# Hybrid decoder block on one core: down-weight sums moved to the up phase, seven down entries taken early, first norm's gains spread by TensorE

## The chip, the core and the metric

The kernel runs on one core of a Trainium2 chip. The metric is the device time of one execution in microseconds. Three runs of the kernel before gave 1432.56, 1430.29 and 1428.49 us; the median is 1430.29 us.

## What is computed

One decoder layer on 1024 tokens of width 1024, with 16 meta tokens put in front (L = 1040). All of it is float32. Cut to what matters here:

```
h  = concat(meta, x)
xn = rmsnorm(h) * g_attn                       # first norm
proj = xn @ w_in                               # q, k, v of 4 differential and 8 stick-breaking heads
h  = h + heads(proj) @ w_out                   # attention, per-head norms, output projection
u  = rmsnorm(h) * g_ffn @ w_up                 # 2 x 2816 columns: gate and up
c  = conv_b + causal depthwise conv3(u)
h  = h + (silu(c_gate) * c_up) @ w_down        # 2816 -> 1024
out = (rmsnorm(h) * g_final)[16:]
```

## The kernel before

Each float32 factor is split into a high part (rounded for the fast matmul) and a low part (the rest); a product is three matmuls, high x high, high x low and low x high. ScalarE makes the high part by a copy, GpSimd or VectorE the low part by a subtraction. All transfers are issued on SyncE's queue. The order of instructions on each engine is fixed when the kernel is built: a list scheduler takes, in a simulation, the instruction traced first among those that are ready, and `tc.issue_after(x)` keeps an instruction behind x on its engine.

**First norm and first projections** (`first_unit`, `first_norm`, L220 to L231). Nine row tiles (a meta tile of 16 rows, eight of 128) are loaded; SyncE loads g_attn broadcast to 128 partitions (512 KB, L372) between them. Each tile gets its square sum (ScalarE, L224), `rstd` (L151 to L156), a multiply by rstd and g_attn, and a transposition with a split into xT_hi and xT_lo (L180, L183, L184). Six tiles are multiplied by one VectorE instruction (L230); tiles 3, 5 and 7 (`POOL_X`) by GpSimd with g_attn (L227) and by VectorE with rstd (L228). The projections of unit 0 (L297) run after tiles 0 to 2, 3 to 5 and 6 to 8. Values are transposed through the two banks of tag "tr".

**Attention phase.** Projection of the next unit and attention of the current one are interleaved by a written planner. `load_w` (L251) loads an input weight into one of two raw buffers and splits it. With the fourth to twelfth weight it also calls `sum_down` (L267), once for each of the nine pairs of down-weight tiles: two loads of 512 KB into the same two raw buffers, four GpSimd subtractions of 512 columns (L274 to L277), two stores of 512 KB into down_sums. These are the sums of weight blocks that a seven-product scheme for a 2 x 2 block product needs.

**Up phase** (loop over ff from 3 to 21, 19 steps). A step computes gate and up columns of one 128-wide tile with the same seven-product scheme: products `a11, a12, s2, s3, s1, a22, s4` (L1063), each 4 x 3 x 2 matmuls of 258 columns. Four weight entries a step are split by `prepare`: `load_up` loads two raw tiles (512 KB each) and forms sums ta and tb on GpSimd (L1041 to L1044); `split_w` makes high (ScalarE, L907) and low part (GpSimd, L908) in three buffers dh, dl. Convolution taps run on ScalarE and VectorE (L915, L917). Gated tiles, and sums of them (`gated_sums`, L1093 to L1099), are stored as blocks (L1087).

**Down phase.** After the last step's gates (`rest`, `gated_sums`) the pools are closed, the bank pool psd and the pool ph opened, and twelve entries taken. `take(k)` loads 256 KB of blocks and 256 KB of weight (from w_down or down_sums, L1181, L1182) into one of eight raw buffers, copies the high part (L1189), and subtracts the low part, half on GpSimd, half on VectorE (L1191). Entries 0 to 2 of each twelve use dh and dl, the others eh and el in ph. Three pairs form a group; a chain of 36 matmuls of 512 columns (L1221) uses three entries, the group's first chain entry by entry, and after each chain three more are taken. Four plain rows and the last norm follow (L1239, L1243).

Of the kernel before, what the change touches and what calls it, by code (L numbers as in the profile page):

```python
# [44 lines left out]
SUMS_FROM = 4  # L45
# [7 lines left out]
POOL_X = (3, 5, 7)  # L53
# [16 lines left out]
def f(ap):  # L70
    return ap.bitcast(F32)
# [25 lines left out]
def hybrid_block(ctx: ExitStack, tc: tile.TileContext, x, meta, g_attn, w_in, lq1, lk1, lq2, lk2,  # L97
# [8 lines left out]
    def bank(tag):  # L106
        return psum.tile([P, 512], F32, tag=tag, name=f"ps_{tag}", bufs=2)
# [89 lines left out]
    down_sums = dram.tile([N_PAIRS, 2, P, D], F32, name="down_sums")  # L197
# [12 lines left out]
    gb = pr.tile([P, D], F32, tag="aT", name="g_attn_b", bufs=3)  # L210
    rows = {}

# [6 lines left out]
    def first_norm(t):  # L219
        t0, n = tok_span(t)  # L220
        xt = rows[t]
        ss = pr.tile([P, 1], F32, tag="ss", name="ss", bufs=4)
        junk = pn.tile([P, D], BF16, tag="yb", name="junk")
        nc.scalar.activation(junk[:n], xt[:n], AF.Square, accum_out=ss[:n])  # L224
        r = rstd(pr, ss[:n], n, "rs")
        if t in POOL_X:
            nc.gpsimd.tensor_tensor(xt[:n], xt[:n], gb[:n], op=ALU.mult)  # L227
            nc.vector.tensor_scalar(xt[:n], xt[:n], r, None, op0=ALU.mult)  # L228
        else:
            nc.vector.scalar_tensor_tensor(xt[:n], xt[:n], r, gb[:n], op0=ALU.mult, op1=ALU.mult)  # L230
        transpose_split(xt, n, [(xT_hi, xT_lo, t0, 0)], ("s", "av"))  # L231
# [19 lines left out]
    def load_w(src):  # L251
        raw = pw.tile([P, D], F32, tag="raw", name="raw", bufs=2)
        nc.sync.dma_start(raw, src)
        if len(w_taken) == 2:
            both = pk_odd.tile([P, 2, D], F32R, tag="k", name="w_v0")
            hi, lo = both[:, 0], both[:, 1]
        else:
            hi = pw.tile([P, D], F32R, tag="wh", name="wh", bufs=2)
            lo = pw.tile([P, D], F32R, tag="wl", name="wl", bufs=2)
        w_taken.append(1)  # L260
        nc.scalar.copy(hi, raw)
        nc.gpsimd.tensor_tensor(lo, raw, f(hi), op=ALU.subtract)
        if 0 <= len(w_taken) - SUMS_FROM < N_PAIRS:
            sum_down(len(w_taken) - SUMS_FROM)
        return hi, lo

    def sum_down(p):  # L267

        ff = N_ROWS + 2 * p
        r0, r1 = (pw.tile([P, D], F32, tag="raw", name="raw", bufs=2) for _ in range(2))  # L270
        for i, r in enumerate((r0, r1)):
            nc.sync.dma_start(r, w_down[P * (ff + i) : P * (ff + i + 1), :])
        b11, b12, b21, b22 = (r[:, 512 * h : 512 * h + 512] for r in (r0, r1) for h in range(2))
        nc.gpsimd.tensor_tensor(b11, b12, b11, op=ALU.subtract)  # L274
        nc.gpsimd.tensor_tensor(b12, b22, b12, op=ALU.subtract)
        nc.gpsimd.tensor_tensor(b22, b22, b11, op=ALU.subtract)
        nc.gpsimd.tensor_tensor(b21, b21, b22, op=ALU.subtract)  # L277
        for i, r in enumerate((r0, r1)):
            nc.sync.dma_start(down_sums[p, i], r)
# [86 lines left out]
    def first_unit():  # L366
# [5 lines left out]
        nc.sync.dma_start(gb, g_attn.broadcast_to([P, D]))  # L372
# [529 lines left out]

    def split_w(pool, tags, src, bufs):
        hi = pool.tile([P, D], F32R, tag=tags[0], name=tags[0], bufs=bufs)
        lo = pool.tile([P, D], F32R, tag=tags[1], name=tags[1], bufs=bufs)
        w = src.shape[-1]
        nc.scalar.copy(hi[:, :w], src)  # L907
        nc.gpsimd.tensor_tensor(lo[:, :w], src, f(hi)[:, :w], op=ALU.subtract)  # L908
        return hi, lo
# [191 lines left out]

    prepare(0)
    prepare(1)
    rest = sums_of = before = None
    for ff in range(PLAIN, NF):
# [4 lines left out]
        prepare(k + 2)  # L1110
        w = ready.pop(k)
# [17 lines left out]
        prepare(k + 4)  # L1129
        w = ready.pop(k + 2)  # L1130
# [7 lines left out]
        if sums_of:  # L1138
            gated_sums(*sums_of)
            sums_of = None  # L1140
        prepare(k + 5)
# [13 lines left out]
    silus = rest()  # L1155
    gated_sums(*sums_of)
    banks.close()
    left_s.close()
# [3 lines left out]
    psd = banks.enter_context(tc.tile_pool(name="psd", bufs=1, space=PSUM, reuse_waits="tile"))  # L1162
# [6 lines left out]
    taken = {}  # L1169

    def take(k):
# [5 lines left out]
        if q < N_PAIRS:  # L1177
            ff = N_ROWS + 2 * q
            b11, b12, b21, b22 = (w_down[P * r : P * (r + 1), cs] for r in (ff, ff + 1) for cs in (lower, upper))
            t1, t3, t4, t2 = (down_sums[q, r, :, cs] for r in range(2) for cs in (lower, upper))  # L1180
            nc.sync.dma_start(raw[:, lower], blocks[q, i])  # L1181
            nc.sync.dma_start(raw[:, upper], (b11, b21, t2, t3, t1, t4, b22)[i])  # L1182
        else:
            ff = q - N_PAIRS
            nc.sync.dma_start(raw, w_down[P * ff : P * (ff + 1), :] if i else gated[ff])
        pool, tags, bufs = (pd, ("dh", "dl"), 3) if k % ENTRIES < 3 else (ph, ("eh", "el"), ENTRIES - 3)
# [18 lines left out]
    for k in range(ENTRIES):  # L1205
        take(k)
    with tc.issue_after(silus[0].ins), tc.issue_after(silus[1].ins):
        nc.scalar.preload_act_table_set("natural_log_exp_and_others")
# [80 lines left out]
```

## Time and profile before

| | |
|---|---|
| median of three runs | 1430.29 us (1428.49 to 1432.56) |
| the profiled execution's own time | 1427.61 us |
| its span | 1425.9 us |
| mean granted TensorE clock | 0.985 |
| TensorE matmul busy | 1347.5 us (95%) |
| VectorE busy | 967.8 us (68%) |
| ScalarE busy | 714.9 us (50%) |
| GpSimd busy | 749.2 us (53%) |
| share of the chain that ended last | TensorE 66%, VectorE 9% |

The span runs from the first to the last instruction; the 1.7 us between it and the execution's own time lie around it. Busy times are sums over each engine's instructions. In the rows, PE is TensorE's matmul, PEld its weight load, DVE VectorE, ACT ScalarE, POOL GpSimd, SP SyncE (SPq its queue of transfers). L numbers are lines of the kernel. A granted clock of 1.00 is 2.4 GHz, 0.50 is 1.2 GHz.

### The profile page before, as it was taken

Reading aid. Unit: us, or ns where it says so; the run is one execution under the profiler, and the core shown is the slowest. Engines: PE = TensorE matmul, PEld = TensorE weight load, DVE = VectorE, ACT = ScalarE, POOL = GpSimd, SP = SyncE. Lnnn points to the kernel's source line nnn. Section 1 sums busy time; section 2 is a strip of 40 time slices with the busy share of each in tenths; the row PEclk is TensorE's granted clock in tenths of the full one; section 3 lists DMA queues with packets and bytes.
Section 4 is the critical chain, followed back from the end, with each engine's and each line's share of the span. In section 5 each row is a group of like instructions: output and inputs, shape, how many; then the busy total and the mean of one; then the engine's idle time right before and its main releaser. Section 6 shows DMA issues by size and latency. Waiting matters only on the chain.

```text
span 1425.9 us, 24695 instructions
## 1 busy us (share of the span) xinstructions
PE 1347.5 (95%) x9000; PEld 1251.1 (88%) x9000; DVE 967.8 (68%) x1816; ACT 714.9 (50%) x1406; POOL 749.2 (53%) x769
## 2 busy tenths in 40 slices
PE   5999989999998998899999899999999996999997
PEld 5989989998987887678899899999999995888886
DVE  7377867778676787875877546555555565977755
ACT  6355655666575666542444344444454444534322
POOL 5145444235666676852103367766776573966620
PEclk9999999999999999999999999999999998999999
DMA  5154454221211127335633222323223325966502
GB/s 215 52 184 153 151 162 144 60 68 38 60 43 40 46 59 224 84 73 140 169 122 129 78 82 92 110 97 104 77 94 97 111 91 202 325 203 191 177 15 104
DMA packets 93569, 166.35 MB, mean 117 GB/s; under 512 B 11628, under 2 KB 46060, under 8 KB 93448
## 3 DMA queue, kind: packets, MB, share of 16 engines
q1 hardware_dynamic: 93448, 164.78, 37.0%
q8 instruction: 71, 1.16, 0.4%
q14 instruction: 50, 0.41, 0.1%
HBM read 111.49 MB, written 44.85 MB: 110 GB/s over the span
## 4 chain that ended last, share of the span: by engine, by line
PE 66%; DVE 9%; issue 4%; ACT 3%; POOL 2%; DMA 1%; SPq 0%; DVEq 0%; POOLq 0%; ACTq 0%
PE x L1063 27%; PE ps_x L1221 7%; PE ps_mm L297 7%; PE ps_y L1221 5%; PE ps_mm L745 5%; DVE s L501 3%; PE ps_av L588 2%; PE ps_tr L559 2%; PE ps_s L927 2%; PE ps_av L927 2%; PE ps_x L1239 2%; PE ps_y L1239 2%; PE ps_s L444 1%; PE ps_s L445 1%; PE ps_tr L180 1%
## 5 line engine op out<-in xcount | busy, mean ns | idle before, releaser
L297 PE MATMUL ps_mm<-xT_hi,wh 128*128 128x342 f32 (+7 forms) x552 | 182.6, 331 | 4.7 <-DVE qz L307 3.2
L297 PE MATMUL ps_mm<-xT_lo,wh 128*128 128x342 f32 (+7 forms) x552 | 180.1, 327 | 0.2 <-DVE xT_lo L184 0.2
L297 PE MATMUL ps_mm<-xT_hi,wl 128*128 128x342 f32 (+7 forms) x552 | 179.2, 326 | 0.0
L588 PE MATMUL ps_av<-aT,v 128*128 128x256 f32 (+3 forms) x608 | 130.8, 306 | 4.7 <-POOL aT L566 4.1
L908 POOL TENSOR_TENSOR dl<-raw,dh 128x1024 fp32r<-128x1024 f32 (+1 forms) x43 | 82.8, 1926 | 95.3 <-ACT dh L907 95.3
L1063 PE MATMUL x<-yh,dl 128*128 128x258 f32 x608 | 124.2, 286 | 0.0
L1063 PE MATMUL x<-yh,dh 128*128 128x258 f32 x608 | 123.7, 285 | 0.0
L1063 PE MATMUL x<-yl,dh 128*128 128x258 f32 x608 | 123.6, 285 | 0.0
L501 DVE TENSOR_TENSOR_SCAN s<-s 128x912 f32<-128x912 f32 (+6 forms) x72 | 100.3, 1396 | 21.8 <-POOL s L497 19.8
L1069 ACT COPY kept<-x 128x516 f32<-128x516 f32 x76 | 44.8, 590 | 135.2 <-PE x L1063 135.2
L297 PEld LDWEIGHTS ps_mm<-xT_hi,wh 128*128 128x128 f32 x552 | 105.5, 191 | 7.9 <-issue 2.4
L559 PE MATMUL ps_tr<-ident,a 128*128 128x128 f32 (+1 forms) x540 | 92.9, 277 | 18.8 <-DVE o L671 6.1
L1191 POOL TENSOR_TENSOR el<-down_raw,eh 128x512 fp32r<-128x512 f32 x53 | 91.3, 1753 | 35.9 <-ACT eh L1189 35.9
L588 PEld LDWEIGHTS ps_av<-aT,v 128*128 128x128 f32 (+2 forms) x608 | 95.2, 190 | 14.4 <-POOL aT L566 4.5
L297 PEld LDWEIGHTS ps_mm<-xT_lo,wh 128*128 128x128 f32 x552 | 105.6, 191 | 1.0 <-DVE xT_lo L184 0.5
L297 PEld LDWEIGHTS ps_mm<-xT_hi,wl 128*128 128x128 f32 x552 | 105.4, 191 | 0.3
L502 POOL TENSOR_TENSOR a<-a,s 128x912 f32<-128x912 f32 (+3 forms) x64 | 83.6, 1308 | 41.0 <-DVE s L501 33.6
L571 DVE TENSOR_TENSOR aT<-ps_tr,aT 128x512 fp32r<-128x512 f32 (+3 forms) x132 | 76.4, 585 | 34.2 <-ACT aT L570 33.4
L1063 PEld LDWEIGHTS x<-yh,dh 128*128 128x128 f32 x608 | 95.3, 191 | 0.0
L1063 PEld LDWEIGHTS x<-yl,dh 128*128 128x128 f32 x608 | 95.0, 191 | 0.0
L1063 PEld LDWEIGHTS x<-yh,dl 128*128 128x128 f32 x608 | 95.0, 191 | 0.0
L570 ACT CAST aT<-ps_tr 128x512 fp32r<-128x512 f32 (+3 forms) x132 | 66.6, 510 | 50.5 <-PE ps_tr L559 47.8
(306 smaller groups left out, 4057.5 us busy)
## 6 DMA issues: line engine op xcount, KB each, us to landing
raw<-in_w_up SPq DMA_DIRECT2D x44, 512.0 KB, 3.6
down_raw<-blocks SPq DMA_DIRECT2D x63, 256.0 KB, 3.8
raw<-in_w_in SPq DMA_DIRECT2D x24, 512.0 KB, 3.7
blocks<-cg SPq DMA_DIRECT2D x45, 256.0 KB, 3.5
raw<-in_w_down SPq DMA_DIRECT2D x18, 512.0 KB, 3.8
down_sums<-raw SPq DMA_DIRECT2D x18, 512.0 KB, 2.9
down_raw<-down_sums SPq DMA_DIRECT2D x36, 256.0 KB, 4.3
down_raw<-in_w_down SPq DMA_DIRECT2D x27, 256.0 KB, 4.1
```

What stands on the lines that cost most here:

```text
L297: nc.tensor.matmul(ps[:, :w], a[:, kt * P : (kt + 1) * P], b[:, kt, c0 : c0 + w], start=(kt == 0 and i == 0), stop=(kt == KT - 1 and i == 2))
L501: nc.vector.tensor_tensor_scan(s[:n, rev], s[:n, rev], s[:n, rev], 1.0, op0=ALU.mult, op1=ALU.bypass)
L502: (nc.gpsimd if t else nc.vector).tensor_tensor(b[:n, :keys], b[:n, :keys], s[:n, 1 : keys + 1], op=ALU.mult)
L559: pe_last[0] = nc.tensor.transpose(ps[:kn, at : at + qn], a[:qn, kk0 : kk0 + kn], ident[:qn, :qn])
L570: nc.scalar.copy(aT[:kn, 0, f0:end], ps[:kn, f0:end])
L571: nc.vector.tensor_tensor(aT[:kn, 1, f0:end], ps[:kn, f0:end], f(aT)[:kn, 0, f0:end], op=ALU.subtract)
L588: pe_last[0] = nc.tensor.matmul(av[:, :w], v[:kn, kt, vi, :], aT[:kn, ai, j * w : (j + 1) * w], start=job["count"] == 0, stop=job["count"] ...
L745: nc.tensor.matmul(ps[:n], a, b[:, hs], start=(j == 0 and i == 0), stop=(j == len(wo) - 1 and i == 2))
L908: nc.gpsimd.tensor_tensor(lo[:, :w], src, f(hi)[:, :w], op=ALU.subtract)
L1063: nc.tensor.matmul(x[:, s], w[a][:, ks], y[b][:, kt, SUB * s : SUB * s + SUB + 2], start=start and kt == 0 and i == 0, stop=kt == KT // 2 ...
L1191: engine.tensor_tensor(lo[:, cs], raw[:, cs], f(hi)[:, cs], op=ALU.subtract)
L1221: nc.tensor.matmul(ps, a[:, P * t : P * (t + 1)], b[:, upper], start=begin and j == 0 and i == 0, stop=j == n - 1 and i == 2, skip_group_c ...
```

## The change

- `sum_down` and its call go. A class `DownSums` makes the same sums in the up phase, one half of a pair (256 of 512 columns) to a step, for the 18 steps ff = 3 to 20: it loads four blocks of 128 x 256 (128 KB each) at the step's start, subtracts on GpSimd behind the split of entry k + 4, and stores four blocks before `prepare(k + 5)`. Its four buffers are those of tag "o" in pn. down_sums becomes [pair, 4, 128, 512].
- The down entries 0 to 6 (`EARLY = 7`) are taken before the last `rest` and `gated_sums`. Only right_f (the y tiles) is closed ahead of them, so ph, with the eight raw buffers and four eh and el, lies where the y tiles lay. The other five buffers (ih, il) go to a pool pi, opened on the left where the up phase's sums lay, after the last gates. The bank pool psd is opened behind all twelve.
- g_attn is loaded as one row; two float32 matmuls with a row of ones spread it into the two "tr" banks, where it stays until tile 8 is normed. All nine tiles are multiplied on VectorE, in two halves of 512 columns, each transposed behind its half.

```diff
+    def spread_gains():
+        row = pr.tile([1, D], F32, tag="aT", name="g_attn_row", bufs=3)
+        nc.sync.dma_start(row, g_attn)
+        one = pr.tile([1, P], F32, tag="vT", name="one_row", bufs=2)
+        nc.vector.memset(one, 1.0)
+        for h in range(2):
+            ps = bank("tr")
+            nc.tensor.matmul(ps, one, row[:, 512 * h : 512 * h + 512], start=True, stop=True)
+            gains.append(ps)
...
-        if t in POOL_X:
-            nc.gpsimd.tensor_tensor(xt[:n], xt[:n], gb[:n], op=ALU.mult)
-            nc.vector.tensor_scalar(xt[:n], xt[:n], r, None, op0=ALU.mult)
-        else:
-            nc.vector.scalar_tensor_tensor(xt[:n], xt[:n], r, gb[:n], op0=ALU.mult, op1=ALU.mult)
-        transpose_split(xt, n, [(xT_hi, xT_lo, t0, 0)], ("s", "av"))
+        for h, tag in enumerate(("s", "av")):
+            hs, ks = slice(512 * h, 512 * h + 512), slice(4 * h, 4 * h + 4)
+            nc.vector.scalar_tensor_tensor(xt[:n, hs], xt[:n, hs], r, gains[h][:n], op0=ALU.mult, op1=ALU.mult)
+            transpose_half(xt[:, hs], n, [(xT_hi[:, ks], xT_lo[:, ks], t0, 0)], tag)
...
-        if 0 <= len(w_taken) - SUMS_FROM < N_PAIRS:
-            sum_down(len(w_taken) - SUMS_FROM)
...
-        nc.sync.dma_start(gb, g_attn.broadcast_to([P, D]))
+        spread_gains()
...
+    class DownSums:
+        def __init__(self, step):
+            p, h = divmod(step, 2)
+            self.cols = slice(SUB * h, SUB * h + SUB)
+            self.out = down_sums[p]
+            self.b = [pn.tile([P, 342], F32, tag="o", name="b", bufs=4)[:, :SUB] for _ in range(4)]
+            for i, b in enumerate(self.b):
+                r, c = divmod(i, 2)
+                at = HD * c + SUB * h
+                nc.sync.dma_start(b, w_down[P * (N_ROWS + 2 * p + r) : P * (N_ROWS + 2 * p + r + 1), at : at + SUB])
+        def add(self):
+            b11, b12, b21, b22 = self.b
+            nc.gpsimd.tensor_tensor(b11, b12, b11, op=ALU.subtract)
+            nc.gpsimd.tensor_tensor(b12, b22, b12, op=ALU.subtract)
+            nc.gpsimd.tensor_tensor(b22, b22, b11, op=ALU.subtract)
+            nc.gpsimd.tensor_tensor(b21, b21, b22, op=ALU.subtract)
+        def store(self):
+            for i, b in enumerate(self.b):
+                nc.sync.dma_start(self.out[i, :, self.cols], b)
...
         prepare(k + 2)
+        down = DownSums(ff - PLAIN) if ff - PLAIN < 2 * N_PAIRS else None
...
         prepare(k + 4)
+        if down:
+            with tc.issue_after(split_last[0].ins):
+                down.add()
...
+        if down:
+            down.store()
         prepare(k + 5)
...
-    silus = rest()
-    gated_sums(*sums_of)
-    banks.close()
-    left_s.close()
     right_f.close()
...
-        pool, tags, bufs = (pd, ("dh", "dl"), 3) if k % ENTRIES < 3 else (ph, ("eh", "el"), ENTRIES - 3)
+        at = k % ENTRIES
+        pool, tags, bufs = (pd, ("dh", "dl"), 3) if at < 3 else (ph, ("eh", "el"), EARLY - 3) if at < EARLY else (pi[0], ("ih", "il"), ENTRIES - EARLY)
...
-    for k in range(ENTRIES):
+    for k in range(EARLY):
         take(k)
+    silus = rest()
+    gated_sums(*sums_of)
+    banks.close()
+    left_s.close()
+    pi.append(ctx.enter_context(tc.tile_pool(name="pi", bufs=1, side="left", reuse_waits="tile")))
+    for k in range(EARLY, ENTRIES):
+        take(k)
+    psd = banks.enter_context(tc.tile_pool(name="psd", bufs=1, space=PSUM, reuse_waits="tile"))
```

## Rows read from the trace of the kernel before

**Rows 1.** TensorE's waits over the span: who for whom, us total, times, longest.

```profile
PE ps_x L1221 <- ACT dh L1189: 13.0, 1, 13.0
...
PE ps_av L588 <- POOL aT L566: 4.1, 2, 2.8
...
PE ps_tr L559 <- DVE a L479: 2.5, 1, 2.5
```

**Rows 2.** Windows: stretch and length, busy us per engine (instructions), clock, DMA, GB/s.

```profile
8.00:37.00 29.00, 20.75 (x131) 19.61 (x132) 27.69 (x61) 20.77 (x51) 18.84 (x9) 1.00 0.53 198
...
60.00:240.00 180.00, 171.16 (x1147) 165.51 (x1146) 131.82 (x379) 98.49 (x224) 86.94 (x87) 0.99 0.51 161
...
850.00:1187.00 337.00, 337.00 (x2784) 337.00 (x2783) 189.22 (x263) 162.93 (x231) 220.46 (x128) 1.00 0.29 95
1187.40:1200.50 13.10, 0.09 (x1) 0.00 (x0) 6.66 (x12) 3.62 (x4) 0.00 (x0) 0.68 0.57 203
1200.50:1211.00 10.50, 10.48 (x36) 8.48 (x37) 7.25 (x7) 7.03 (x7) 9.69 (x6) 0.76 1.03 375
1211.00:1374.00 163.00, 163.00 (x721) 134.97 (x720) 128.05 (x148) 63.15 (x64) 112.27 (x66) 1.00 0.62 199
```

**Rows 3.** Chain that ended last, first down chains: start, us, what.

```profile
1200.52 10.83 PE ps_x L1221 x36
1211.35 8.16 PE ps_y L1221 x36
```

**Rows 4.** Timeline at the seam of up and down phase: start, us, engine, instruction.

```profile
1195.59 0.38 SPq L1181 DMA_DIRECT2D down_raw<-blocks  x1
...
1199.42 1.04 ACT L1189 CAST dh<-down_raw 128x1024 fp32r<-128x1024 f32 x1 [8.56 <-DMA down_raw<-in_w_down]
```

**Rows 5.** Timeline of the first norm and first projections.

```profile
7.06 1.27 DVE L230 SCALAR_TENSOR_TENSOR xt<-xt,rs,g_attn_b 16x1024 f32<-16x1024 f32 x1 [0.71 <-DMA g_attn_b<-in_g_attn]
...
10.33 1.12 PE L180 MATMUL ps_s<-ident,xt 128*128 128x128 f32 x4 [0.85 <-DVE rs L153]
...
11.75 2.64 DVE L230 SCALAR_TENSOR_TENSOR xt<-xt,rs,g_attn_b 128x1024 f32<-128x1024 f32 x1
...
16.64 2.82 DVE L228 TENSOR_SCALAR xt<-xt,rs 128x1024 f32<-128x1024 f32 x1 [0.32 <-POOL xt L227]
...
21.20 0.58 PE L297 MATMUL ps_mm<-xT_lo,wh 128*128 128x272 f32 x1
...
46.20 0.26 ACT L329 CAST v<-ps_tr 16x128 fp32r<-16x128 f32 x1
46.21 1.12 DVE L307 SCALAR_TENSOR_TENSOR qz<-ps_mm,qz 64x384 fp32r<-64x384 f32 x2 [3.10 <-ACT qz L305]
```

**Rows 6.** Transfers by issue: count, KB each, median us to landing.

```profile
gated<-c SPq DMA_DIRECT2D x12, 128.0 KB, 1.8
```

**Rows 7.** Timeline of GpSimd in the attention phase, near 205 us.

```profile
204.67 1.26 POOL L277 TENSOR_TENSOR raw<-raw 128x512 f32<-128x512 f32 x1
206.00 0.73 POOL L566 CAST aT<-aT 16x256 fp32r<-16x256 f32 x2
```

**Rows 8.** Timeline of one up step: GpSimd, SyncE's queue and TensorE.

```profile
1019.89 2.42 POOL L908 TENSOR_TENSOR dl<-raw,dh 128x1024 fp32r<-128x1024 f32 x1
1023.71 2.42 POOL L908 TENSOR_TENSOR dl<-tb,dh 128x1024 fp32r<-128x1024 f32 x1
...
1024.99 0.41 PE L1063 MATMUL x<-yh,dl 128*128 128x258 f32 x2
...
1031.02 1.29 POOL L908 TENSOR_TENSOR dl<-raw,dh 128x512 fp32r<-128x512 f32 x1 [2.55 <-ACT dh L907]
...
1031.05 0.41 PE L1063 MATMUL x<-s2h,dl 128*128 128x258 f32 x2
...
1032.34 0.33 SPq L685 DMA_DIRECT2D raw<-in_w_up  x1
...
1036.69 1.33 POOL L1041 TENSOR_TENSOR ta<-raw 128x512 f32<-128x512 f32 x1 [4.38 <-issue]
```

More of the change, by code (lines that the diff above doesn't have):

```diff
@@ L44 @@
 STAGED = 8
-SUMS_FROM = 4
+EARLY = 7
 B_EARLY = 0
@@ L52 @@
 OUT_A, OUT_B, OUT_C = range(0, 3), range(3, 6), range(6, 8)
-POOL_X = (3, 5, 7)
 COL = 0.4219
@@ L196, in hybrid_block @@
     blocks = dram.tile([N_PAIRS, 7, P, HALF], F32, name="blocks")
-    down_sums = dram.tile([N_PAIRS, 2, P, D], F32, name="down_sums")
+    down_sums = dram.tile([N_PAIRS, 4, P, HALF], F32, name="down_sums")
     left, left_out, right, right_a, right_b = (ExitStack() for _ in range(5))
@@ L209, in hybrid_block @@
     xT_lo = pl.tile([P, KT, L], F32R, name="xT_lo")
-    gb = pr.tile([P, D], F32, tag="aT", name="g_attn_b", bufs=3)
+    gains = []
     rows = {}
+    def spread_gains():
[7 more added lines that the diff above has]
+            gains.append(ps)
     def load_rows(ts_):
@@ L262, in load_w @@
         nc.gpsimd.tensor_tensor(lo, raw, f(hi), op=ALU.subtract)
-        if 0 <= len(w_taken) - SUMS_FROM < N_PAIRS:
-            sum_down(len(w_taken) - SUMS_FROM)
         return hi, lo
[L267 to L279, printed above, removed]
     w_src, w_ready, w_taken = w_in_tiles(), [], []
@@ L900, in second_norm @@
             transpose_split(yn, m, places, ("tr", "tr"))
+    split_last = [None]
     def split_w(pool, tags, src, bufs):
@@ L907, in split_w @@
         nc.scalar.copy(hi[:, :w], src)
-        nc.gpsimd.tensor_tensor(lo[:, :w], src, f(hi)[:, :w], op=ALU.subtract)
+        split_last[0] = nc.gpsimd.tensor_tensor(lo[:, :w], src, f(hi)[:, :w], op=ALU.subtract)
         return hi, lo
@@ L1154, in hybrid_block @@
         before = cg
-    silus = rest()
-    gated_sums(*sums_of)
-    banks.close()
-    left_s.close()
     right_f.close()
-    psd = banks.enter_context(tc.tile_pool(name="psd", bufs=1, space=PSUM, reuse_waits="tile"))
     ph = ctx.enter_context(tc.tile_pool(name="ph", bufs=1, side="right", reuse_waits="tile"))
@@ L1168, in hybrid_block @@
     steps += [(i, N_PAIRS + r) for r in range(N_ROWS) for i in range(2)]
-    taken = {}
+    taken, pi = {}, []
     def take(k):
@@ L1179, in take @@
             b11, b12, b21, b22 = (w_down[P * r : P * (r + 1), cs] for r in (ff, ff + 1) for cs in (lower, upper))
-            t1, t3, t4, t2 = (down_sums[q, r, :, cs] for r in range(2) for cs in (lower, upper))
+            t1, t3, t4, t2 = (down_sums[q, r] for r in range(4))
             nc.sync.dma_start(raw[:, lower], blocks[q, i])
```

## The prediction

> **What bounds the kernel now.** Three views were read. The list of TensorE's waits [rows 1] names one long wait, 13.0 us, before the first matmul of the down projection; everything else is a few microseconds. The windows [rows 2] give each stage its limit. From 8 to 37 us VectorE is busy 27.69 of 29.00 us: the first norm hangs on it. From 60 to 240 us TensorE works 171.16 of 180.00 us, so 8.8 us are lost. In the up phase TensorE is busy 337.00 of 337.00 us at clock 1.00, and GpSimd only 220.46. Between 1187.4 and 1200.5 it does nothing, its clock falls (0.68, then 0.76), and from 1211 it is full again. The chain [rows 3] prices the fall: the first 36 down matmuls take 10.83 us, the next 36 take 8.16, so 2.7 us. The timeline of the seam [rows 4] says why: the first down loads are issued at 1195.59, behind the last blocks on SyncE's queue, and the first split starts at 1199.42.
>
> **Part 1, down entries loaded early.** Seven of the twelve entries are traced ahead of the last gates. Their staging and most of their buffers lie where the four y tiles lay. A step is 168 matmuls, 20.3 us by [rows 2] (337.00 / 2784 x 168), in seven products of 2.9 us. The first y half is last read by product 2, so raw loads can start about 14.5 us before the last product ends. Entry 0 takes a dh buffer freed after product 4, entry 1 after product 6, entry 2 only after product 7. An entry costs a ScalarE copy of 1.04 us [rows 4] and on GpSimd half a split of 1.70 us (112.27 / 66, [rows 2]), with VectorE's half beside it. Entry 0 is ready 5 us early and entry 1 at about the end of the last product; the first chain multiplies entry by entry, 2.7 us each, so entry 2 is needed 5.4 us after that end and is there after 3. The first chain's four banks lie on the first two pairs of the last step, both drained before it ends. The later entries come at 1.7 us of GpSimd each against 2.7 us of TensorE. So the gap goes with its clock loss: 13.0 + 2.7 = 15.7 us. I take 15.0, with 0.7 left for a late second half of entry 1; bounds 11 (one entry's load and split left in the open, some 4.7 us) and 15.7. Late next is the last pair's blocks, stored behind fourteen more loads on SyncE; they are read over 100 us later.
>
> **Part 2, first norm.** A 512 KB broadcast goes, a 4 KB row, a memset, and two fp32 matmuls of 512 columns come. At the 375 GB/s of [rows 2] the broadcast held back what follows on the queue (third row tile, first weights, small inputs) by 1.4 us. The three GpSimd multiplies go, so VectorE no longer runs beside them: two of its instructions took 2.64 and 2.82 us there, the unhindered one 1.27 [rows 5]. In their place each of nine tiles takes two instructions of 512 columns out of PSUM; from the 384-column pair (1.12 us for two, [rows 5]) I estimate 0.69 us, 1.38 a tile. The two crowded tiles give 2.7 us back, the other seven cost about 1.2: net 1.5. The gains need a landing of about 2 us (the 128 KB store's 1.8, [rows 6]) and the matmuls: four fp32 transposes, 512 columns together, took 1.12 us [rows 5], so 2.2 for two, or 4.5 if a product costs twice a transpose. I take 2.2, since the transposes are the only fp32 columns here; the first multiply stands at 7.06 us, so this is covered, and if not it costs 2. Both ps_tr banks stay occupied until tile 8 is normed, which the value transposes, first read after 46 us [rows 5], do not feel. Sum 1.4 + 1.5 = 2.9, taken as 3; bounds -1 and 5 (TensorE's steady start at 21.20 moved up by all of VectorE's backlog).
> The Trainium skill (FP8 and Floating Point Precision, TensorE Precision Notes) says true FP32 goes through the array in four passes. An estimate by it: four times the 0.227 us of one 512-column matmul, 1.8 us for both at full clock and 3.6 at half; by the latter the sum would be 1 us smaller. No row here shows such a product.
>
> **Part 3, sums leave the attention phase.** Nine sets go: 36 GpSimd subtractions of 1.26 us and more, 36 transfers of 512 KB, and their hold on the two raw buffers that the input weights use. At 204.67 a subtraction stands ahead of the cast at 206.00 [rows 7] for which TensorE waited; the two such waits are 4.1 us [rows 1] and go. Of the other 4.7 us lost between 60 and 240 some follows from late weights (I count the 2.5 us behind VectorE's a among it, [rows 1]). I take 5.0. Bounds: 8.8 (all of it) and -2 (nothing, since later stretches may be bound by VectorE's chain, and a changed order of issue may open a new wait).
>
> **Part 4, sums enter the up phase.** Each of 18 steps gains four loads and four stores of 128 KB and four GpSimd subtractions of 256 columns. Between 512 columns (1.29) and 1024 (2.42) [rows 8] a column costs 2.2 ns, so 256 cost 0.73 us, 2.9 a step. They are queued behind the first split of the next tile, which ends at 1022.31, and ahead of the tb split, which starts at 1023.71 and ends at 1026.13; TensorE first reads that low half at 1031.05. So 4.9 us of room take 2.9. The ta split behind it slides into the 2.55 us for which GpSimd idles before 1031.02; some 0.4 us is left over, which moves the second raw load (1032.34) and then the next first split by as much, of 2.7 us of room (1022.31 against 1024.99). On SyncE eight issues of 0.33 us make 2.6 of 20.3; the stores wait for the subtractions, and what stands behind them (blocks, the next first raw load) is not urgent. The bytes add some 51 GB/s to 95. Cost taken: 0, hidden by TensorE's products. Without that cover it is 18 times what exceeds the room; the ends are 0 and the 15 us of the last rival below.
>
> **The sum.** 15 + 3 + 5 - 0 = 23. The profiled execution took 1427.61 us, so 1404.6; the median of the three runs is 2.7 us above it, and against 1430.29 the forecast is 1407. Its own range is 1400 (30 us of gain, all parts near their upper ends) to 1417 (11 from part 1, 2 from the others).
>
> **Rivals.** *Early work does not reach the end.* The attention phase alternates between VectorE, GpSimd and TensorE, and may reabsorb parts 2 and 3; for it speaks that its order of issue changes, against it that TensorE is nearly full from 60 to 240. Only part 1 is left: 1430 - 15 = 1415. Chance 0.15.
> *The early entries are not early.* If ScalarE's copies queue behind its last gates, or SyncE's loads behind the last stores, part or all of the 13 us stays: 1412 with 5 us left, 1422 with all (parts 2 and 3 alone). For it: engines run their queues in order. Against it: the loads are traced first. Chance 0.12.
> *Slower: the second raw load comes late.* Its place is GpSimd's subtraction that starts at 1036.69, after 4.38 us of waiting for this load [rows 8]. If the eight new transfers sit in front of it, they cost 2.6 us of issue and, 1 MB at 375 GB/s, 2.8 us of transfer: 5.4 late, 3.1 beyond the 2.3 us of room, in 18 steps 56 us: 1463. It decides against the change from 3.6 us of delay (23 / 18 = 1.3 beyond the room). Against it: the stores follow the subtractions early in a step, the load comes 8 us into it, and a 128 KB store with short rows lands in 1.8 us. Chance 0.07.
> *The subtractions are blocked by VectorE.* In the first norm both engines together doubled an instruction (2.64 against 1.27). If each of the four waited out a VectorE instruction of 0.7 us, 2.9 would become 5.7, 0.8 beyond the 4.9 of room, 15 us in 18 steps: 1422. Chance 0.03, as VectorE mostly reads PSUM there. The Trainium skill has this as a rule (SBUF - State Buffer, Who interferes with whom): an instruction of VectorE with two SBUF inputs and a reading one of GpSimd shut each other out. By that rule it bites only beside the gates' multiplies, and the rows of the first norm agree.
>
> **How the numbers follow.** The forecast keeps 0.63. The measurement tells about 0.3% (4.3 us) from no change. All cases but the slow one lie below that, save their tails: faster 0.88, same 0.05, slower 0.07. The range runs from 1398 (all upper bounds, 5 + 8.8 + 15.7, give 1401; the three runs spread by some 2 us to either side) to 1422, which takes in the first two rivals and the last.
>
> **What would show it.** Right: no wait of TensorE over 2 us at the seam, clock 1.00 there, the first 36 down matmuls in about 8.2 us; no cast waiting behind subtractions near 206 us; steady projections before 19 us; a full TensorE through the up phase with GpSimd near 80%. Wrong: idle time of TensorE in each up step, a first split later than the step's third matmul pair, or the wait at the seam still above 5 us.

## The result: 3.2% slower, and the profile after

The changed kernel takes 1477.25 us (median of four runs, 1472.25 to 1478.12) against 1429.59 us before on the same chip: a ratio of 1.0323, 95% interval 1.0305 to 1.0342. The forecast was 1407. Its profiled execution took 1477.66 us, with a span of 1475.9 us.

Where the time lies is read best by cutting each span at two places: the first start of a product's matmul in the up phase, and the last start of one (by the rows `x<-s4h,dh` of the product's line; the product's other matmuls follow within a microsecond).

| | start of up phase | up phase | rest |
|---|---|---|---|
| before (span 1425.9) | 799.0 | 387.7 | 239.2 |
| after (span 1475.9) | 780.7 | 460.9 | 234.3 |
| difference | -18.3 | +73.2 | -4.9 |
| forecast | -8 | 0 | -15 |

So what was to come from the first norm and the attention phase came, and more than twice over; the seam gave a third of its share; and the up phase, priced at nothing, lost 73 us. Three windows of the profile after, the same stretches as in [rows 2]:

```profile
8.00:37.00 29.00, 25.93 (x158) 22.79 (x157) 25.54 (x69) 20.51 (x51) 9.13 (x5) 1.00 0.51 184
60.00:240.00 180.00, 179.79 (x1243) 175.48 (x1242) 134.33 (x421) 106.64 (x249) 41.30 (x58) 1.00 0.22 62
...
850.00:1187.00 337.00, 294.74 (x2267) 288.02 (x2266) 215.10 (x217) 130.64 (x188) 213.73 (x159) 0.96 0.39 124
```

TensorE does 25.93 us of work in the stretch of the first norm (before 20.75) and is full from 60 to 240 us. From 850 to 1187 us, where it was full before, it works 294.74 of 337.00 us. GpSimd is not busier there than before (213.73 against 220.46), although each step has a fifth more for it: it waits. TensorE's waits after, as in [rows 1]:

```profile
PE x L1057 <- DVE cu L911: 25.0, 13, 2.4
PE x L1057 <- POOL dl L902: 22.2, 25, 2.5
...
PE ps_tr L220 <- DMA g_attn_row<-in_g_attn: 4.7, 1, 4.7
```

The products wait for low halves (GpSimd's dl) and for banks that a convolution has still to read (VectorE's cu); none of these stood in the list before. All waits of the up phase come to 49.6 us of the 73.2. The other 24 are matmuls that run longer: TensorE is busy 412.16 us in the phase, before 387.90 for as many matmuls, and the granted clock is 0.96, before 1.00. Behind both waits stand two groups of instructions, first before and then after: VectorE's gate multiply, and the first subtraction (ta) that GpSimd makes of a step's second raw tile. Columns: busy us, mean ns of one, idle us of the engine before them and what ended it.

```profile
L1073 DVE TENSOR_TENSOR cg<-cg,cu 128x512 f32<-128x512 f32 x38 | 29.9, 787 | 46.1 <-ACT cg L1072 44.2
...
L1041 POOL TENSOR_TENSOR ta<-raw 128x512 f32<-128x512 f32 x19 | 25.1, 1321 | 78.4 <-DMA raw<-in_w_up 57.7 <-issue 19.4 <-DVE sb L980 1.4
```

```profile
L1067 DVE TENSOR_TENSOR cg<-cg,cu 128x512 f32<-128x512 f32 x38 | 111.8, 2942 | 93.9 <-ACT cg L1066 92.1
...
L1035 POOL TENSOR_TENSOR ta<-raw 128x512 f32<-128x512 f32 x19 | 24.9, 1313 | 148.2 <-DMA raw<-in_w_up 119.0 <-issue 27.8 <-DVE sb L974 1.4
```

The multiply takes 2942 ns on the mean instead of 787. GpSimd's wait for the second raw tile grows from 78.4 to 148.2 us in all, by 69.8 us, nearly the whole loss of the up phase. One step, first in the profile before (to add to [rows 8]: the start of its ta, and the gate multiply), then in the profile after; lines of GpSimd, VectorE and SyncE's queue:

```profile
1016.09 1.33 POOL L1041 TENSOR_TENSOR ta<-raw 128x512 f32<-128x512 f32 x1 [4.12 <-DMA raw<-in_w_up]
...
1028.84 0.69 DVE L1073 TENSOR_TENSOR cg<-cg,cu 128x512 f32<-128x512 f32 x1 [2.49 <-ACT cg L1072]
```

```profile
1013.18 1.32 POOL L1035 TENSOR_TENSOR ta<-raw 128x512 f32<-128x512 f32 x1 [10.79 <-DMA raw<-in_w_up]
...
1022.66 2.39 POOL L902 TENSOR_TENSOR dl<-tb,dh 128x1024 fp32r<-128x1024 f32 x1
...
1024.12 5.78 DVE L1067 TENSOR_TENSOR cg<-cg,cu 128x512 f32<-128x512 f32 x1 [6.50 <-ACT cg L1066]
1025.02 0.73 POOL L1113 TENSOR_TENSOR b<-b 128x256 f32<-128x256 f32 x1
1025.71 2.39 POOL L902 TENSOR_TENSOR dl<-ta,dh 128x1024 fp32r<-128x1024 f32 x1
...
1026.60 2.59 SPq L1106 DMA_DIRECT2D b<-in_w_down  x2
1028.07 1.28 POOL L902 TENSOR_TENSOR dl<-raw,dh 128x512 fp32r<-128x512 f32 x1
...
1031.93 0.70 DVE L1067 TENSOR_TENSOR cg<-cg,cu 128x512 f32<-128x512 f32 x1
...
1032.65 0.33 SPq L1081 DMA_DIRECT2D blocks<-cg  x1
1033.08 0.38 SPq L677 DMA_DIRECT2D raw<-in_w_up  x1
1036.53 1.31 POOL L1035 TENSOR_TENSOR ta<-raw 128x512 f32<-128x512 f32 x1 [7.18 <-DMA raw<-in_w_up]
```

Read the step after by its ends. GpSimd's instructions follow each other without a pause until 1029.35; the multiply that began at 1024.12 ends at 1029.90, when they do, and the next one, with GpSimd idle, takes 0.70. At 1029.35 the last split of the tile is done and its raw buffer free, but the load that refills it is issued at 1033.08: on SyncE's queue it stands behind a block store that waits for that second multiply (1031.93 + 0.70 = 1032.63). Its data is there 3.4 us later, and only then does GpSimd's next row begin. From 852 us on every one of 15 steps is like this: the load is issued 2.4 to 4.3 us after the split that frees its buffer, 58.8 us in all, where before it was 0.03 us behind it. The rest of the 69.8 us is slower landing.

Three theories fit this picture. **P**: the held multiply itself starves TensorE of banks. **Q**: the eight added transfers hold the raw load back. **R**: the loss runs round a loop (GpSimd's row, the raw load, the next row), in which every microsecond by which the load is late is lost in each step. P and Q were on record before the halves of the moved sums were run; R was added after gap (below) had been measured, before the two kernels that test it were built.

### The profile page after: what moved, and what is told of

Its sections match the earlier page's. It is cut to its first block, busy times and chain, and to the rows that moved or that the text cites. A ratio compares the mean times of both kernels' runs of the same rounds, so it can differ in the third digit from the quotient of the medians.

```text
span 1475.9 us, 24961 instructions
## 1 busy us (share of the span) xinstructions
PE 1371.9 (93%) x9004; PEld 1262.3 (86%) x9004; DVE 1031.7 (70%) x1826; ACT 712.6 (48%) x1406; POOL 733.7 (50%) x802
## 4 chain that ended last, share of the span: by engine, by line
PE 60%; issue 12%; DVE 11%; DMA 7%; POOL 4%; ACT 4%; SPq 1%; POOLq 0%; DVEq 0%; ACTq 0%
PE ps_mm L289 14%; PE x L1057 11%; PE ps_x L1248 6%; PE ps_mm L737 5%; PE ps_y L1248 4%; PE ps_av L580 4%; PE ps_tr L551 3%; DMA raw<-in_w_up 3%; DVE s L493 2%; POOL dl L902 2%; PE ps_s L921 2%; PE ps_s L436 2%; PE ps_s L437 2%; PE ps_av L921 2%; DVE cu L911 2%
## 5 line engine op out<-in xcount | busy, mean ns | idle before, releaser
L289 PE MATMUL ps_mm<-xT_hi,wh 128*128 128x342 f32 (+6 forms) x552 | 181.6, 330 | 1.7 <-DVE qz L299 1.0
L289 PE MATMUL ps_mm<-xT_lo,wh 128*128 128x342 f32 (+6 forms) x552 | 179.2, 325 | 0.0
L289 PE MATMUL ps_mm<-xT_hi,wl 128*128 128x342 f32 (+6 forms) x552 | 178.7, 325 | 0.0
L1067 DVE TENSOR_TENSOR cg<-cg,cu 128x512 f32<-128x512 f32 x38 | 111.8, 2942 | 93.9 <-ACT cg L1066 92.1
L1057 PE MATMUL x<-yh,dl 128*128 128x258 f32 x608 | 127.7, 292 | 17.8 <-POOL dl L902 17.8
L1035 POOL TENSOR_TENSOR ta<-raw 128x512 f32<-128x512 f32 x19 | 24.9, 1313 | 148.2 <-DMA raw<-in_w_up 119.0
```

Of the source, the lines that this page charges most:

```text
L289: nc.tensor.matmul(ps[:, :w], a[:, kt * P : (kt + 1) * P], b[:, kt, c0 : c0 + w], start=(kt == 0 and i == 0), stop=(kt == KT - 1 and i == 2))
L1057: nc.tensor.matmul(x[:, s], w[a][:, ks], y[b][:, kt, SUB * s : SUB * s + SUB + 2], start=start and kt == 0 and i == 0, stop=kt == KT // 2 ...
L1067: nc.vector.tensor_tensor(cg[:, h], cg[:, h], cu[:, h], op=ALU.mult)
```

## The experiments

**First the parts, each alone.** The edits are the change's own: the first norm (only_norm), the early down entries (only_early), both of these (norm_early), and the sums moved (only_move).

> The first norm's change alone (gains spread by TensorE, multiplies on VectorE out of PSUM), the rest as in the kernel before. Both theories of the up phase leave it alone. If the 18.4 us by which the changed kernel starts its up phase earlier come mainly from here, the time is 8 us or more below before (under 1422); by the prediction's term it is 3 below (1427). The attention phase keeps its two waits of 4.1 us for the cast behind the subtractions.

> The seven early down entries alone; sums in the attention phase and first norm as before. Both theories: the up phase keeps 388 us, the seam's 13.0 us wait falls below 3 us and the first down chain comes near 8.2 us, so 12 to 15 us less: 1415 to 1418. If it saves under 8, the early entries themselves wait for something.

> First norm and early entries together, sums left in the attention phase. Both theories: the up phase keeps 388 us, and the gains of the two single parts add: 1400 to 1415, the fastest so far.

> The sums moved to the up phase alone. Both theories: the up phase grows from 388 to 460 us or more, against 5 to 10 us gained in the attention phase, so 1490 to 1505. If the up phase stays near 388, the loss needs the early entries or the earlier start too, and both theories fall.

| | median us | ratio to before (95%) | start of up phase | up phase | rest |
|---|---|---|---|---|---|
| only_norm | 1420.67 | 0.9940 (0.9920 to 0.9961) | 792.1 | 388.9 | 240.0 |
| only_early | 1422.00 | 0.9954 (0.9938 to 0.9971) | 798.8 | 387.7 | 233.6 |
| norm_early | 1416.59 | 0.9912 (0.9895 to 0.9928) | 793.4 | 389.0 | 233.1 |
| only_move | 1485.36 | 1.0392 (1.0368 to 1.0415) | 788.0 | 457.1 | 239.4 |

The loss belongs to the moved sums alone, which also start the up phase 11.0 us earlier (5 to 10 expected, so only_move came out under the 1490 to 1505 expected). The other two parts gain 6.8 and 8.1 us alone. Two expectations missed: only_early should have gained 12 to 15, and the gains do not add, since norm_early gains 12.2 and not 14.9.

**Then the halves of the moved sums.** In no_subtract the four subtractions are left out, so the sums in the down projection are plain copies of weight blocks. In no_transfers the subtractions work on four tiles loaded once, nothing is stored, and the down entries read plain weights.

```diff
@@ no_subtract @@
-        if down:
-            with tc.issue_after(split_last[0].ins):
-                down.add()
@@ no_transfers @@
-            for i, b in enumerate(self.b):
+            for i, b in enumerate(self.b if first else ()):
...
-        if down:
-            down.store()
```

> Leaves out the four subtractions of each up step (GpSimd's added work); the four loads and four stores of a step stay, so the sums in the down projection are plain copies of the weights. Theory P (GpSimd's added instructions close the gap in which VectorE's gate multiply, with two SBUF inputs, could run): the gate multiply falls from a mean of 2.9 us to about 0.7, the up phase from some 465 us back to about 388, and the time to 1400 to 1412, since parts 1 and 2 and the empty attention phase remain. Theory Q (eight added transfers a step hold the second raw load back on SyncE's queue): the up phase stays near 465 us and the time near 1477, with GpSimd idle longer before the ta subtraction.

> Keeps the four subtractions of each up step but on tiles that are loaded once; the loads and stores of the steps are left out, and the down entries read plain weights where they read sums. Theory P: the gate multiply still takes about 2.9 us on the mean, the up phase stays above 440 us and the time above 1450. Theory Q: the second raw load is on time again, the up phase takes about 388 us and the time is 1400 to 1412. Something between, near 1435, would say that both are needed.

Neither theory alone: no_subtract takes 1425.21 us (up phase 405.2), no_transfers 1420.28 (404.4). The halves cost 17.5 and 16.7 us, both together 73.2. In no_transfers the multiply is held as before, at 2721 ns, yet the loss is less than a quarter, so P alone is out. In no_subtract, with nothing between loads and stores, the order built for SyncE puts all 18 sets between 769.5 and 882.3 us, and the loss lies there; it says that transfers ahead of raw loads cost time, but not what they cost where the changed kernel has them. One step of no_transfers:

```profile
1019.02 6.50 DVE L1066 TENSOR_TENSOR cg<-cg,cu 128x512 f32<-128x512 f32 x1 [2.65 <-ACT cg L1065]
...
1023.62 1.35 POOL L901 TENSOR_TENSOR dl<-raw,dh 128x512 fp32r<-128x512 f32 x1
...
1026.81 0.33 SPq L1080 DMA_DIRECT2D blocks<-cu  x1
1027.24 0.37 SPq L676 DMA_DIRECT2D raw<-in_w_up  x1
```

With the multiply held and no added transfers, the raw load is still 2.3 us late here (1027.24 against 1024.97), behind block stores; but so it is in every second step only, and in the others it is issued at once.

**Then the place of the subtractions.** The gap kernel makes them behind the last split of the tile (entry k + 3), while GpSimd waits for the raw load anyway; vector_adds makes them on VectorE.

```diff
         prepare(k + 3)
+        if down:
+            with tc.issue_after(split_last[0].ins):
+                down.add()
...
         prepare(k + 4)
-        if down:
-            with tc.issue_after(split_last[0].ins):
-                down.add()
```

> The four subtractions stand behind the split of entry k+3 instead of entry k+4, so in front of, not behind, the stretch in which GpSimd waited for its next raw tile. Theory P: the row of GpSimd's instructions without a break gets shorter where the first gate multiply falls; that multiply returns to near 0.7 us unless another VectorE instruction with two SBUF inputs meets the subtractions, and the up phase loses at most half of what it loses now: 400 to 430 us, time 1415 to 1440. Theory Q: the stores are ready earlier but as many; the up phase stays near 465 us and the time near 1477.

> The four subtractions of each step are done by VectorE instead of GpSimd; GpSimd has its idle stretches back. Theory P: the gate multiply is back near 0.7 us, but the four subtractions have two SBUF inputs too and must find gaps in GpSimd's row themselves, so part of the loss stays: up phase 395 to 440 us, time 1410 to 1450. Theory Q: transfers are as many as now, the up phase stays near 465 us and the time near 1477.

gap takes 1403.62 us, a ratio of 0.9824 (0.9806 to 0.9843): 1.8% faster than the kernel before, with as many transfers on the same queue, and better than both theories expected. The transfers as such (Q) are therefore not enough for the loss. Its up phase is 388.8 us, so the moved sums cost nothing there. vector_adds takes 1445.91 (1.0115, 1.0100 to 1.0130; up phase 428.8). It came out in the range that P gave, but not by P's reason: its multiply is back at 727 ns, but VectorE now waits in its own order for the loaded blocks, 41.0 us in all before the first two subtractions (28.8 + 12.2): a queue blocked by a transfer again, on another engine.

gap doesn't tell P from R, since the new place both opens the pause for the multiply and takes the subtractions out of the loop. **Two kernels cut the loop and leave the subtractions where the change put them.** u_on_pool issues the second raw load on GpSimd's own queue, right behind the split that frees the buffer; third_half loads that tile in two halves and gives the half that is read last a second buffer.

```diff
@@ u_on_pool @@
-        g, u = load_raw(w_up[ff]), load_raw(w_up[NF + ff])
+        g, u = load_raw(w_up[ff]), pw.tile([P, D], F32, tag="raw", name="raw", bufs=2)
+        nc.gpsimd.dma_start(u, w_up[NF + ff])
@@ third_half @@
...
+        u_lo, u_hi = v[:, lo], other if ff % 2 else v[:, hi]
+        nc.sync.dma_start(g, w_up[ff])
+        nc.sync.dma_start(u_lo, w_up[NF + ff][:, lo])
+        nc.sync.dma_start(u_hi, w_up[NF + ff][:, hi])
...
```

> The changed kernel, but the second raw load of a step is issued on GpSimd's own queue, directly behind the split that frees its buffer, instead of on SyncE's queue behind stores and block stores. Theory R (the lost time runs round a loop: GpSimd's row of a step without a break, then the issue and landing of the second raw load, then the next row; the late gate multiply and the added transfers only lengthen it through SyncE's order): the wait before the ta subtraction falls from 7 to 11 us to some 4 us, a step from 25 us to about 21.5, and the time from 1477 to 1410 to 1430, although the gate multiply is still held for several microseconds. Theory P (the held gate multiply itself keeps TensorE waiting for banks): a step stays above 24 us and the time above 1460.

> The changed kernel, but the half of the second raw tile that is read last (by the fourth split) gets two buffers, so that its load no longer waits for the end of GpSimd's row; the tile is loaded in two halves. Transfers, subtractions and their order on GpSimd stay. Theory R: the loop is cut, the up phase takes 388 to 395 us and the time is 1400 to 1412, although the gate multiply is still held (mean above 2 us). Theory P: the gate multiply still keeps TensorE waiting, the up phase stays above 440 us and the time above 1450. If the loads still stand behind late block stores in SyncE's order, something between: 400 to 430 us, 1415 to 1445.

u_on_pool takes 1412.72 us (0.9884, 0.9853 to 0.9914; up phase 395.3), third_half 1403.87 (0.9827, 0.9797 to 0.9857; up phase 388.3). The two groups of u_on_pool, then three lines of one of its steps:

```profile
L1068 DVE TENSOR_TENSOR cg<-cg,cu 128x512 f32<-128x512 f32 x38 | 100.8, 2654 | 34.9 <-ACT cg L1067 33.0
...
L1036 POOL TENSOR_TENSOR ta<-raw 128x512 f32<-128x512 f32 x19 | 25.5, 1341 | 8.2 <-DMA raw<-in_w_up 3.7 <-PE x L1058 3.2 <-DVE sb L974 1.4
```

```profile
1017.47 4.71 DVE L1068 TENSOR_TENSOR cg<-cg,cu 128x512 f32<-128x512 f32 x1 [2.51 <-ACT cg L1067]
...
1022.04 0.58 POOL L1032 DMA_DIRECT2D raw<-in_w_up  x1 [0.41 <-POOL dl L902]
...
1022.21 0.33 SPq L1082 DMA_DIRECT2D blocks<-cg  x1
```

Here the multiply is held as in the changed kernel (2654 ns on the mean) and the transfers are all there, but the wait before ta is 8.2 us in all instead of 148.2, and 65.6 of the 73.2 us are back. The block store still comes late, at 1022.21, behind the held multiply; the raw load no longer stands behind it. Not all of the wait is gone, for GpSimd's order changed too: the next tile's first split now stands ahead of ta and takes over part of it (after, then u_on_pool):

```profile
L902 POOL TENSOR_TENSOR dl<-raw,dh 128x1024 fp32r<-128x1024 f32 x24 | 57.2, 2384 | 48.1 <-ACT dh L901 48.1
```

```profile
L902 POOL TENSOR_TENSOR dl<-raw,dh 128x1024 fp32r<-128x1024 f32 x24 | 58.8, 2453 | 97.7 <-ACT dh L901 97.7
```

That is why the wait before ta is 0.4 us a step and not the 4 expected. TensorE, which decides the time, waits 3.4 us for banks in the whole phase and no longer for GpSimd's halves. This decides for R against P: a held multiply alone leaves at most 395.3 - 388.8 = 6.5 us. The same two groups for third_half:

```profile
L1076 DVE TENSOR_TENSOR cg<-cg,cu 128x512 f32<-128x512 f32 x38 | 48.7, 1282 | 46.1 <-ACT cg L1075 44.3
...
L1044 POOL TENSOR_TENSOR ta<-raw 128x512 f32<-128x512 f32 x19 | 33.0, 1735 | 1.5 <-DVE sb L974 1.4
```

The loop is gone (1.5 us of wait) and so is the loss. My expectation that the multiply would stay above 2 us was a miss: freed from the load, GpSimd's row came out in another order, with pauses, and the multiply fell to 1282 ns. And for gap, where both are cured:

```profile
L1067 DVE TENSOR_TENSOR cg<-cg,cu 128x512 f32<-128x512 f32 x38 | 29.8, 783 | 46.1 <-ACT cg L1066 44.2
...
L1035 POOL TENSOR_TENSOR ta<-raw 128x512 f32<-128x512 f32 x19 | 25.1, 1321 | 8.0 <-DMA raw<-in_w_up 6.6 <-DVE sb L974 1.4
```

**Last, the seam.** In only_early SyncE issues the first early load in time and the next one 9 us later, and the first chain of 36 matmuls starts at 1187.36 and ends at 1200.49, 13.1 us for 8.2 us of work, with these loads and waits:

```profile
1175.52 0.38 SPq L1177 DMA_DIRECT2D down_raw<-blocks  x1
1175.95 0.45 SPq L1178 DMA_DIRECT2D down_raw<-in_w_down  x1
1184.85 0.32 SPq L1177 DMA_DIRECT2D down_raw<-blocks  x1
...
1187.36 0.50 PE L1226 MATMUL ps_x<-dh 128*128 128x512 f32 x1
1189.28 0.50 PE L1226 MATMUL ps_x<-dl,dh 128*128 128x512 f32 x1 [1.42 <-DVE dl L1188]
...
1191.29 0.47 PE L1226 MATMUL ps_x<-dh 128*128 128x512 f32 x1 [1.28 <-DVE cu L918]
```

```profile
1187.36:1200.49 13.13, 10.43 (x37) 7.93 (x37) 13.13 (x14) 8.76 (x9) 10.37 (x7) 0.87 1.00 359
```

The two waits make 2.7 us of the excess of 4.9. The rest is matmuls that run longer: the last line, the window of the chain with columns as in [rows 2], has 10.43 us of them at a granted clock of 0.87. VectorE is busy in all of the 13.13 us.

The reason for the 9 us stands in the layout of the built program: the second raw buffer lies at bytes 152,800 to 156,896 of a partition, and the second half of the y tiles begins at 156,768. By 128 bytes the load must wait until TensorE has read that half, in the sixth of the last seven products, and all loads behind it wait with it. gap_pad is gap with a tile of 256 bytes at the end of that pool, which moves the buffers clear; pad_banks also exchanges the two sets of banks of the first chains.

```diff
@@ gap_pad @@
     for k in range(EARLY):
         take(k)
+    ph.tile([P, 64], F32, tag="pad", name="pad")
@@ pad_banks @@
+    first_y = [bank_of("y") for _ in range(half_nt)]
...
+                chains[tag] = first_y if k == n and tag == "y" and group is groups[0] else [bank_of(tag) for _ in range(half_nt)]
```

> The gap kernel with 256 bytes a partition added at the end of the pool of the early entries. In the kernels so far the second raw buffer of that pool reaches 128 bytes into the second half of the y tiles, which TensorE reads until the sixth of the last seven products, and every load behind it waits with it on SyncE's queue. Expected by this theory: the second and later early loads are issued about 9 us earlier, right behind the first; the waits of the first down chain for low halves go, and the time falls by 3 to 8 us below the gap kernel's, to 1396 to 1400. By the rival, that ScalarE's and VectorE's own order at the seam (copies behind the last convolutions, subtractions behind the last gates) sets the first chain: within 2 us of the gap kernel.

> The gap_pad kernel with the two sets of banks of the first down chains exchanged: the first chain's four banks then lie where the pairs z and y of the last step were, and not where x and v, the last product's pair, were. If the banks hold the first chain back, as the wait of 1.3 us for the last convolution of cu says: that wait goes, the first chain gets some 1.5 us shorter and the time is 1400 to 1402, beside 1402.7. By the rival, that the first entries' late splits (ScalarE's copies behind the last convolutions) decide, the wait only moves to the next split: within 1 us of 1402.7.

gap_pad takes 1402.71 us (0.9818, 0.9787 to 0.9849; rest 232.9), pad_banks 1402.36 (0.9828, 0.9815 to 0.9842; rest 233.2). The loads do come 8.4 us earlier (the second 0.94 us behind the first, in gap 9.33), and the time is within 1 us of gap's: both expectations that named a cause of the seam missed in the time, and the rivals held. Of gap_pad, its loads, the first copy, and the window of the first chain:

```profile
1157.15 0.38 SPq L1199 DMA_DIRECT2D down_raw<-blocks  x1
...
1158.09 0.42 SPq L1199 DMA_DIRECT2D down_raw<-blocks  x1
...
1167.22 0.78 ACT L909 ACTIVATE cg<-x,cb,cw 128x512 f32<-128x512 f32 x1 [1.46 <-DVE x L1156]
1167.90 1.03 ACT L1208 CAST dh<-down_raw 128x1024 fp32r<-128x1024 f32 x1
...
1168.90:1185.00 16.10, 12.97 (x46) 9.75 (x47) 16.09 (x17) 8.39 (x10) 11.19 (x7) 0.89 0.58 201
```

The copy of entry 0 stands in ScalarE's order behind a convolution that waits for VectorE, and VectorE is busy 16.09 of the 16.10 us. In pad_banks the first chain is down from gap_pad's 13.1 us to 9.0 (its first matmul starts at 1169.7, the next chain's at 1178.7), as expected and more, but the waits move ahead of it and into the second, at VectorE's halves of later entries:

```profile
PE ps_y L1250 <- DVE el L1210: 2.8, 2, 2.4
PE ps_x L1250 <- DVE cg L911: 1.5, 1, 1.5
```

The rest of the span is 232.8 to 234.3 us in every kernel with early entries, whatever was done to loads, banks or the up phase. That VectorE's work sets it is argued from its full window and from the rivals that fell; no kernel here takes work off VectorE at the seam. gap_pad and pad_banks are the fastest kernels tried, 1.8 and 1.7% below the one before; they, gap and third_half can't be told apart.

## Why the prediction was wrong, step by step

**Part 4 failed.** Its words were "Cost taken: 0, hidden by TensorE's products"; it was 73.2 us. The durations were right (the subtractions took 0.73 to 0.75 us each, 0.73 estimated). Three steps of the argument were not.

- "some 0.4 us is left over, which moves the second raw load (1032.34) and then the next first split by as much, of 2.7 us of room (1022.31 against 1024.99)." The row itself did not get longer: from ta to the end of the fourth split it takes 16.2 us before and after (1016.09 to 1032.31, 1013.18 to 1029.35). But the room was counted as if it were met once, and the path closes on itself: ta of one step to the end of the fourth split, then the raw load, then ta of the next. Before, ta starts at 1016.09 and again at 1036.69, 20.6 us apart, of which 4.38 us are the load [rows 8]; TensorE's step is 20.3. The loop had no room but the 2.55 us that the subtractions filled, and any delay of the load is paid in every step. GpSimd waited 69.8 us more for it in all.
- "what stands behind them (blocks, the next first raw load) is not urgent." The urgent one was the second raw load, and it stood behind the blocks.
- That GpSimd's 2.55 us of pause were free for the taking. VectorE's gate multiply ran in that pause before (at 1028.84, between the splits that end at 1028.48 and start at 1031.02); with the pause filled, it took 5.78 us in the step shown, the block store waited for it, and the raw load for the store. The last rival had the mechanism, but priced it as a delay of GpSimd's subtractions; the delay fell on VectorE. The Trainium skill (SBUF — State Buffer, Who interferes with whom) says that the reads of a GpSimd instruction and a VectorE instruction with two SBUF inputs exclude each other. The traces agree, and add that the exclusion can last over several GpSimd instructions on end: 0.70 us with GpSimd idle, 5.78 beside an unbroken row. The prediction's "only beside the gates' multiplies" is too narrow: the block sums of `gated_sums` have two SBUF inputs as well.

The rival *Slower: the second raw load comes late* was what happened, at the place that it named (1036.69 there, 1036.53 after) and near its price (1463, measured 1477). That the price is near is partly luck: it was made of the issue and transfer of the eight transfers in front of the load, and what stood in front in the step shown was a block store that waited for the multiply. The 0.07 was too small because "the stores follow the subtractions early in a step" was weighed for the added transfers only, and not for what those share the queue with. The held multiply without the added transfers makes 16.7 us of the 73.2 (no_transfers). What the added loads and stores alone would make in the changed kernel's order was not separated: the kernels that free the multiply also take the load off the path or change the order.

**Part 1 was mis-sized**: 15.0 forecast, 6.8 measured alone (only_early), below the lower bound of 11. The wait of 13.0 us went, but not its clock loss: the first chain took 13.1 us, with a granted clock of 0.87, and the next three took 27.5 us instead of 24.5. Later chains and plain rows are some 2 us slower together (a chain takes up to 8.43 us instead of 8.16); why, no run shows. What came instead looks like a seam bound by VectorE, of which no term spoke: it makes half of every low part, finishes the gates and makes the block sums, all within the first chain. "The first y half is last read by product 2, so raw loads can start about 14.5 us before the last product ends" was wrong for all but the first, by 128 bytes; "The first chain's four banks lie on the first two pairs of the last step, both drained before it ends" was wrong for two of them (the wait of 1.28 us); mending both bought nothing that can be measured.

**Part 2 was mis-sized the other way**: 3 forecast, 8.1 measured (1428.79 - 1420.67), above the upper bound of 5; its profiled execution, the slowest of its four, starts the up phase 6.9 us earlier. Steady projections begin at 16.89 us instead of 21.20, as the bound said, but TensorE is also fuller right after: 25.93 against 20.75 us between 8 and 37 us. Which of the two terms, the queue's 1.4 or VectorE's 1.5, was too small, no run separates; the 1.2 that the seven other tiles were to cost is 0.8 by the prediction's own durations (7 x 0.11), so its sum should have been 3.3. Its reading of [rows 1] also passes over a wait of 8.5 us, that of the first transposition, which starts at 8.48 before and at 8.26 after. The halves of the multiply were sized well (0.74 us, 0.69 estimated). The two float32 products were not:

```profile
4.72 3.75 PE L220 MATMUL ps_tr<-g_attn_row,one_row 1*128 1x512 f32 x4 [4.72 <-DMA g_attn_row<-in_g_attn]
```

They took 3.75 us; the transposes had made me take 2.2. It was covered, as argued. The Trainium skill (FP8 and Floating Point Precision, TensorE Precision Notes) gives true float32 four passes, by my estimate 1.8 us for both at full clock and 3.6 at half. The granted clock of this stretch is 1.00 in the profile, so the trace is at twice what the page makes of it there, and the measurement decides. But the same transposition takes 1.11 us just behind the products (at 9.46), and in the kernel before 1.12 at 10.33 [rows 5] and 0.60 later, though the granted clock from 8 to 37 us is 1.00 in both:

```profile
28.47 0.60 PE L180 MATMUL ps_s<-ident,xt 128*128 128x128 f32 x4
```

So the durations of the first stretch fit the lower of TensorE's two levels, whatever the granted clock says, and 3.75 us is near the page's figure at half; why the profile has 1.00, no run here shows.

**Part 3 was mis-sized too**: 5 forecast, 11.0 measured as an earlier start of the up phase (only_move), above the upper bound of 8.8. The window from 60 to 240 us alone gained 8.6 us (171.16 to 179.79), nearly all of the 8.8 that it had lost. Its waits there fall from 8.7 us to 0.2 (before: [rows 1] and smaller ones), those for the casts among them. So more of the other 4.7 us than was taken hung on the moved sums; whether by late weights, no run separates.

Without part 4 the terms would have come to 6.8 + 8.1 + 11.0 = 25.9 us, and gap, the change with its subtractions elsewhere, gains 25.9 (1429.56 - 1403.62). That the two agree to a tenth is chance: two terms are differences of medians, the third is read from single profiled executions, and the first two together gave 12.2 and not 14.9. The forecast of 23 was thus near for a kernel that differs from the one built only in where the four subtractions stand, and near by luck: part 1 was sized at twice what it gave, parts 2 and 3 at less than half.

## What to carry to other kernels

When work is added to an engine, follow its path until it either ends or returns to itself: in a loop, a delay is paid every turn, and the wait for a refill of the buffer that was read last is part of it. Before filling an engine's pause, look at what other engines do in just that pause. And on an in-order queue ask of each urgent transfer what it stands behind, and what that waits for; placing new work inside the wait for the load, not ahead of it, made the same sums free.

## What was not expected of the hardware

A VectorE multiply of 0.70 us took up to 6.50 us (no_transfers, at 1019.02) beside a row of GpSimd instructions that are each no longer than 2.45 us. It ended at 1025.52, when the row did (1024.97): VectorE did not get its turn between them.
